# The first input of a two-network kernel made feature-major ahead of its scale and shift

## The chip, the core and the metric

One core of one Trainium2 chip runs the whole program. The metric is the device time of one execution in microseconds; the kernel before has a median of 1216.44 us over three runs (1214.46 to 1216.67). Everything is fp32; where the kernel multiplies at the faster rate it splits an operand into a high part (`hi`, type fp32r) and the rest (`lo`) and adds three products, `hi*hi + lo*hi + hi*lo`.

## The reference, cut to what matters

A token block of 256 rows and 1024 features goes through seven sublayers. Every sublayer has an input `h` that is a normalised `x`, scaled and shifted by vectors that come from a condition `c` through a 1024-row matrix:

```
shift, scale, gate = split(c @ mod_w[layer, 0] + mod_b[layer, 0], 3)
h = rms_norm(x, norm_w[layer, 0, 0]) * (1.0 + scale) + shift
y = mixer_ab(h, ...)      # first sublayer: h @ w_in, then two attentions
```

The change concerns only the first `h`: `x` is an input, and the scale and shift of this one sublayer (2 x 1024 columns of `mod_w`, 8 MB) have to be read and multiplied with `c` before any projection can start. The scales, shifts and gates of the later sublayers (a 1024 x 1024 matrix each) are made beside other work.

## The kernel before, in words

`start` makes the first `h`, feature-major: `hh` and `hl` (the high and low part) hold 8 blocks of 128 features by 256 tokens. It works in two halves q of 512 features (four blocks each), and in each half first on the scale (v = 0) and then on the shift (v = 1). Row kk of the matrix, as packed, is a 128 x 512 tile; eight rows make one vector half. `load(q, v, i)` brings four of them (i = 0 or 1) by two DMAs. Each row is either multiplied into `acc` by VectorE (`scalar_tensor_tensor`, line 1554) or multiplied on TensorE with `c` spread over 128 columns (`cb`, line 1551); `total` adds `acc` with a matrix of ones (line 1557). So scale and shift come as rows, spread over all partitions. `scaled` multiplies `x` with the scale (tokens on partitions); `shifted` adds the shift, turns the result by eight transposes per half (line 1579) and splits it into `hh` and `hl` (lines 187 and 188).

The first projection is the query of the second attention (`ab_qb`). It too works by halves: `prepare(i, t)` splits a quarter of the weights of half i into `whi` (ScalarE) and `wlo` (VectorE) through `split`; `run(i, t)` multiplies it, 12 products of 128x128 by 256 columns (lines 178 to 180). `run(0, t)` needs the first half of `h` alone, `run(1, t)` the second. The first is issued inside `start`, the second at the start of `mixer_ab`, followed by `ab_kb` and `ab_v` (`tok`), and then the softmax pipeline of the two attentions with further projections as filler. Beside it, in pieces, the gate of the first sublayer and the scale and shift of the second are summed: VectorE's `macc` (line 319), each piece with its own 1 MB DMA of `mod`.

What sets the order: TensorE's instructions run as the program writes them. All others are put in order when the program is built, by a scheduler that plays through estimated times; every engine then runs its list strictly in that order. `issue_after(a)` forbids the scheduler to place an instruction ahead of `a`. All DMAs go through SyncE's one list into one queue. Buffers `raw` (six, 1 MB each) and `whi`/`wlo` (four each) are used in turn.

Of the kernel before, what the change touches and what calls it, by code (L numbers as in the profile page):

```python
# [17 lines left out]
D = 1024  # L18
# [35 lines left out]
def packed(np, I):  # L54
# [75 lines left out]
    o["s5_b"], o["s5_cm"] = b.reshape(128, 1024), ct.reshape(128, 1024)  # L130
    o["mod_bias"] = np.concatenate([I["mod_b"].reshape(12, D), I["b_mod_2"].reshape(9, D)])
# [3 lines left out]
class Net:  # L135
    def __init__(self, ctx, tc, I, out, dbg=None):
        self.ctx, self.tc, self.nc, self.I, self.out, self.dbg = ctx, tc, tc.nc, I, out, dbg or {}
        self.bgq, self.late, self.wait = [], [], 0
        self.anchor = None
# [102 lines left out]
    def split(self, src, shape, pool=None):  # L242
# [13 lines left out]
        self.nc.scalar.activation(hv, src, AF.Copy)  # L256
        self.nc.vector.tensor_tensor(lv, src, hv.bitcast(F32), ALU.subtract)  # L257
# [592 lines left out]
    def mixer_ab(self, hh, hl):  # L850
        nc, I = self.nc, self.I
        with self.tc.tile_pool(name="ab", bufs=1) as ap:
            self.ap = ap
            Tb = [self.bias_load(h0, 3) for h0 in (8, 12)]
# [6 lines left out]
            nc.sync.dma_start(out=sink, in_=I["swa_sinks"][0].partition_broadcast(128))  # L861
# [17 lines left out]
            self.bgq = later  # L879
# [636 lines left out]
    def start(self):  # L1516
# [6 lines left out]
        with self.tc.tile_pool(name="start", bufs=1) as bp:  # L1523
            nw = bp.tile([1, D], F32, name="nw")
            ones = bp.tile([128, 128], F32, name="ones")
            nc.vector.memset(ones, 1.0)
            cb = bp.tile([128, 8, 128], F32, name="cb")
            nc.vector.tensor_copy(cb, self.c1.unsqueeze(2).to_broadcast([128, 8, 128]))
            hh, hl = self.h = self.h_tiles()
            rs = []  # L1530

            def load(q, v, i):

                if i == 0:
                    acc = bp.tile([128, 512], F32, name=f"acc{v}{q}")
                    mods[v] = self.bank([512]), acc, True
                    nc.gpsimd.memset(acc, 0.0)
                ps, acc = mods[v][:2]
                w = I["mod0"][q, v, i]
                r = self.raw() if i == 0 and not (q and v) else bp.tile([128, 2048], F32, name="sraw", bufs=5)  # L1540
                r = r.rearrange("p (k n) -> p k n", k=4)
                pairs = [r[:, 0:2], r[:, 2:4]]
                for k in range(4):
                    kk = 4 * i + k
                    r = pairs[k // 2][:, k % 2, :]
                    if k % 2 == 0:
                        nc.sync.dma_start(out=pairs[k // 2], in_=w[:, k:k + 2])
                        if kk == 0:
                            nc.sync.dma_start(out=acc[0:1, :], in_=I["mod_bias"][1 - v:2 - v, 512 * q:512 * q + 512])
                    if kk in (((1, 3, 5, 7), (1, 3, 5, 7)), ((3, 7), (3, 7)))[q][v]:  # L1550
                        nc.tensor.matmul(ps, cb[:, kk, :], r, start=mods[v][2], stop=False)
                        mods[v] = ps, acc, False
                    else:
                        nc.vector.scalar_tensor_tensor(acc, r, self.c1[:, kk:kk + 1], acc, ALU.mult, ALU.add)

            def total(v):
                nc.tensor.matmul(mods[v][0], ones, mods[v][1], start=False, stop=True)
                return mods[v][0]

            def scaled(q, ts):  # L1560

                sl = slice(512 * q, 512 * q + 512)
                ws = bp.tile([128, 512], F32, name="ws0", bufs=1)
                nb = self.bank([512])
                nc.tensor.matmul(nb, ones[0:1, :], nw[:, sl], start=True, stop=True)
                nc.scalar.activation(ws, nb, AF.Copy)
                nc.vector.scalar_tensor_tensor(ws, total(0), 1.0, ws, ALU.add, ALU.mult)
                for h in range(2):
# [157 lines left out]
```

## Time and profile before

| | |
|---|---|
| median of three runs | 1216.44 us |
| profiled execution | 1219.88 us, its span 1218.1 us |
| busy in the span | TensorE 95%, VectorE 76%, ScalarE 50%, GpSimd 11% |
| mean rate of the DMA queue | 248 GB/s over the span, 412 GB/s from 10 to 45 us |

The span is what the profiler sees between the first and the last instruction. Busy times of different engines overlap; an idle engine costs time only where the next engine waits for it. Matmuls are pipelined, so the length of one (0.28 us) is longer than the distance to the next (0.12 us).

### The profile page before, as it was taken

The page shows a single profiled execution, that of the slowest core. Times are in us where ns is not written, and L with a number is a line of the kernel's source. Part 1 is how long each engine was busy: PE and PEld are TensorE (multiplying, and loading weights), DVE is VectorE, ACT ScalarE, POOL GpSimd, SP SyncE. Part 2 cuts the span into 40 slices and gives each one's busy share as a digit, 9 for nine tenths or more (in the row PEclk, how much of TensorE's full clock was granted, in tenths as well). Part 3 has the DMA queues.
Part 4 walks back from the last instruction along what each step waited for, and adds up shares of the span by engine and source line. Part 5 has one row for each costly group of instructions (what it writes and reads, how often), then busy time and mean ns, then how long its engine had stood idle before and what let it go on. Part 6 is the DMA issues. An engine that isn't in the chain of part 4 may idle for free.

```text
span 1218.1 us, 19252 instructions
## 1 busy us (share of the span) xinstructions
PE 1158.5 (95%) x7460; PEld 1004.7 (82%) x7460; DVE 920.3 (76%) x1352; ACT 603.3 (50%) x1097; POOL 136.2 (11%) x181
## 2 busy tenths in 40 slices
PE   6997999999999999999999799999999889999997
PEld 2885469999878955999988699998888667999985
DVE  5897778877759796997796888777569958666545
ACT  2465545454445654554468764544343324445433
POOL 2000020000000012200000200000028850000000
PEclk9998999999999999999999899999999889999999
DMA  9975578867855768776987488688454534665530
GB/s 351 407 272 191 226 277 313 307 236 301 328 223 221 285 241 350 290 289 253 338 316 267 142 307 312 227 302 339 173 203 148 186 139 173 242 230 190 203 104 34
DMA packets 49537, 302.66 MB, mean 248 GB/s; under 512 B 6155, under 2 KB 6283, under 8 KB 16934
## 3 DMA queue, kind: packets, MB, share of 16 engines
q1 hardware_dynamic: 49446, 301.44, 66.3%
q8 instruction: 58, 0.95, 0.3%
q14 instruction: 33, 0.27, 0.1%
HBM read 295.64 MB, written 5.78 MB: 247 GB/s over the span
## 4 chain that ended last, share of the span: by engine, by line
PE 61%; issue 18%; DVE 10%; DMA 4%; ACT 3%; POOL 3%; POOLq 0%; SPq 0%; DVEq 0%; ACTq 0%
PE ps L180 11%; PE ps L178 11%; PE ps L179 11%; PE y L518 5%; PE y L516 5%; PE y L517 5%; PE y L514 4%; PE tok L546 2%; DMA sraw<-in_mod_dram 2%; DVE macc L319 2%; PE ps L1306 1%; DVE st L1358 1%; ACT p L676 1%; DVE wlo L257 1%; PE ps L432 1%
## 5 line engine op out<-in xcount | busy, mean ns | idle before, releaser
L256 ACT ACTIVATE whi<-raw 128x1024 fp32r<-128x1024 f32 (+2 forms) x307 | 318.1, 1045 | 375.4 <-PE ps L179 148.0
L257 DVE TENSOR_TENSOR wlo<-raw,whi 128x1024 fp32r<-128x1024 f32 (+2 forms) x307 | 370.1, 1211 | 162.8 <-ACT whi L256 161.3
L180 PE MATMUL ps<-hhi,wlo 128*128 128x256 f32 x1488 | 421.9, 284 | 3.4 <-DVE wlo L257 3.4
L178 PE MATMUL ps<-hhi,whi 128*128 128x256 f32 x1488 | 424.2, 285 | 0.0
L179 PE MATMUL ps<-hlo,whi 128*128 128x256 f32 x1488 | 421.5, 283 | 0.0
L180 PEld LDWEIGHTS ps<-hhi,wlo 128*128 128x128 f32 x1488 | 285.9, 192 | 4.4 <-DVE wlo L257 4.4
L178 PEld LDWEIGHTS ps<-hhi,whi 128*128 128x128 f32 x1488 | 285.9, 192 | 2.6 <-issue 1.4
L179 PEld LDWEIGHTS ps<-hlo,whi 128*128 128x128 f32 x1488 | 286.0, 192 | 1.4 <-DVE wlo L257 0.5
L319 DVE SCALAR_TENSOR_TENSOR macc<-raw,c,macc 128x1024 f32<-128x1024 f32 x152 | 194.6, 1280 | 2.4 <-issue 1.5
L516 PE MATMUL y<-whi,gh 128*128 128x512 f32 x352 | 139.6, 397 | 0.0
L518 PE MATMUL y<-whi,gl 128*128 128x512 f32 x352 | 139.1, 395 | 0.0
L517 PE MATMUL y<-wlo,gh 128*128 128x512 f32 x352 | 138.8, 394 | 0.0
L309 POOL MEMSET macc<- 128x1024 f32 x19 | 18.8, 989 | 589.5 <-DVE mlo L334 561.8
L518 PEld LDWEIGHTS y<-whi,gl 128*128 128x128 f32 x352 | 66.5, 189 | 15.4
L517 PEld LDWEIGHTS y<-wlo,gh 128*128 128x128 f32 x352 | 66.6, 189 | 15.2
L516 PEld LDWEIGHTS y<-whi,gh 128*128 128x128 f32 x352 | 66.6, 189 | 14.9
L514 PE MATMUL y<-raw,o 128*128 128x512 f32 x128 | 57.3, 595 | 0.2 <-ACT o L185 0.2
L617 DVE TENSOR_TENSOR g<-sg,ps 128x256 f32<-128x256 f32 x80 | 33.4, 418 | 29.1 <-PE ps L180 29.0
L399 POOL TENSOR_SCALAR ms<-ss 128x1 f32<-128x1 f32 x24 | 11.3, 472 | 372.3 <-ACT junk L409 368.4
L176 PE MATMUL ps<-h,raw 128*128 128x256 f32 x192 | 46.6, 400 | 5.0 <-DVE cvt L1436 5.0
L176 PEld LDWEIGHTS ps<-h,raw 128*128 128x128 f32 x192 | 38.1, 201 | 11.3 <-DVE cvt L1436 5.2
L514 PEld LDWEIGHTS y<-raw,o 128*128 128x128 f32 x128 | 23.4, 190 | 26.6 <-issue 25.6
(313 smaller groups left out, 1439.6 us busy)
## 6 DMA issues: line engine op xcount, KB each, us to landing
raw<-in_mod_dram SPq DMA_DIRECT2D x76, 1024.0 KB
raw<-in_ffn_g_dram SPq DMA_DIRECT2D x44, 1024.0 KB
raw<-in_ffn_u_dram SPq DMA_DIRECT2D x44, 1024.0 KB
raw<-in_ffn_d_dram SPq DMA_DIRECT2D x44, 1024.0 KB
raw<-in_ab_out_dram SPq DMA_DIRECT2D x8, 1024.0 KB
raw<-in_cd_out_dram SPq DMA_DIRECT2D x8, 1024.0 KB
raw<-in_s_c_dram SPq DMA_DIRECT2D x6, 1024.0 KB
raw<-in_s_out_dram SPq DMA_DIRECT2D x6, 1024.0 KB
```

The source lines that it names most:

```text
L176: mm(out, lh, rh, start=first, stop=last)
L178: mm(out, lh, rh, start=first, stop=False)
L179: mm(out, lh, rl, start=False, stop=False)
L180: mm(out, ll, rh, start=False, stop=last)
L256: self.nc.scalar.activation(hv, src, AF.Copy)
L257: self.nc.vector.tensor_tensor(lv, src, hv.bitcast(F32), ALU.subtract)
L319: nc.vector.scalar_tensor_tensor(acc, box["r"][:, kk % 2], c[:, kk:kk + 1], acc, ALU.mult, ALU.add)
L514: mm(ys[h][b], xh[:, k, c], wh[:, 0, sl], start=first, stop=last)
L516: mm(ys[h][b], xh[:, k, c], wh[:, 0, sl], start=first, stop=False)
L517: mm(ys[h][b], xh[:, k, c], wl[:, 0, sl], start=False, stop=False)
L518: mm(ys[h][b], xl[:, k, c], wh[:, 0, sl], start=False, stop=last)
L617: nc.vector.tensor_tensor(g, sg, pu, ALU.mult)
```

## The change

`x` is brought first. ScalarE scales it by its norm alone, TensorE turns it by 16 transposes into `xt` (feature-major) while the weights still arrive. The scale and shift are then wanted as columns: a row of weights is the stationary operand and `c` the moving one, so a product has one column, and four of them (128 features each) make one half. Three rows of eight go this way (`direct`), five are summed by VectorE (`rows`, the first a `tensor_scalar`), and `total` adds that sum with four more one-column products. The bias and the norm weight come as columns too (`cols0`). `modulated` applies scale and shift per partition: ScalarE writes `hh` (Identity with scale and bias), VectorE the same value into `t0` and the difference into `hl`. The splits of `ab_qb` are tied behind the last of these (`heads`). The bias tiles `Tb` and `sink` are loaded after item 4 of `mixer_ab`'s first chain, no longer at its head.

```
-        self.nc.scalar.activation(hv, src, AF.Copy)
-        self.nc.vector.tensor_tensor(lv, src, hv.bitcast(F32), ALU.subtract)
+        with ExitStack() as behind:
+            for a in self.heads:
+                behind.enter_context(self.tc.issue_after(a))
+            self.nc.scalar.activation(hv, src, AF.Copy)
+            self.nc.vector.tensor_tensor(lv, src, hv.bitcast(F32), ALU.subtract)
...
-            Tb = [self.bias_load(h0, 3) for h0 in (8, 12)]
...
                 if i == 4:
                     self.setup()
-            self.bgq = later
+                    nc.sync.dma_start(out=sink, in_=I["swa_sinks"][0].partition_broadcast(128))
+                    Tb = [self.bias_load(h0, 3) for h0 in (8, 12)]
+            self.bgq, self.heads = later, ()
...
+            def column(q, v, lhs, rhs, last=False):
+                for b in range(4):
+                    mm(sums[q][:, 4 * v + b:4 * v + b + 1], lhs[:, 128 * b:128 * b + 128], rhs, start=q not in first,
+                       stop=last and b == 3, skip_group_check=True)
...
+            def rows(q, v, ks):
+                for j, kk in enumerate(ks):
+                    r = parts[q, v, kk // 4][:, kk % 4]
+                    if j == 0:
+                        acc = parts[q, v] = bp.tile([128, 512], F32, name=f"acc{v}{q}")
+                        nc.vector.tensor_scalar(acc, r, self.c1[:, kk:kk + 1], None, ALU.mult)
+                    else:
+                        a = nc.vector.scalar_tensor_tensor(acc, r, self.c1[:, kk:kk + 1], acc, ALU.mult, ALU.add)
+                return a.ins
+            def direct(q, v, kk):
+                column(q, v, parts[q, v, kk // 4][:, kk % 4], self.c1[:, kk:kk + 1])
+            def total(q, v):
+                column(q, v, parts[q, v], one, v == 1)
+                m = bp.tile([128, 4], F32, name=f"m{v}{q}")
...
+            def modulated(q, ws, sh):
+                for b in range(4):
+                    k = 4 * q + b
+                    t = bp.tile([128, 256], F32, name="t0", bufs=3)
+                    nc.vector.tensor_scalar(t, xt[:, k], ws[:, b:b + 1], sh[:, b:b + 1], ALU.mult, ALU.add)
+                    a = nc.scalar.activation(hh[:, k], xt[:, k], AF.Identity, scale=ws[:, b:b + 1], bias=sh[:, b:b + 1]).ins
+                    self.anchor = nc.vector.tensor_tensor(hl[:, k], t, hh[:, k].bitcast(F32), ALU.subtract).ins
+                self.heads = a, self.anchor
...
+            for v in range(2):
+                rows(0, v, (0, 2, 4, 6, 7))
+                for kk in (1, 3, 5):
+                    direct(0, v, kk)
+                mods.append(total(0, v))
+            modulated(0, *mods)
...
-            with self.tc.issue_after(self.anchor):
-                early = {t: prepare(0, t) for t in range(4)}
-            load(1, 0, 0)
-            load(1, 0, 1)
+            early = {t: prepare(0, t) for t in range(4)}
+            fetch(1, 0)
+            fetch(1, 1)
             run(0, 0, early[0])
             run(0, 1, early[1])
-            scaled(1, tb)
-            load(1, 1, 0)
-            load(1, 1, 1)
+            sums[1] = self.bank([8])
+            a = self.anchor
+            for v in range(2):
+                with self.tc.issue_after(a):
+                    a = rows(1, v, (0, 2, 3, 5, 7))
+            direct(1, 0, 1)
             run(0, 2, early[2])
-            shifted(1, tb)
+            direct(1, 0, 4)
             run(0, 3, early[3])
+            direct(1, 0, 6)
+            mods = [total(1, 0)]
+            for kk in (1, 4, 6):
+                direct(1, 1, kk)
+            mods.append(total(1, 1))
+            modulated(1, *mods)
```

The order on VectorE around the moment when `h` is whole, before: `raw_337` is the second half of `ab_qb`, `raw_407` is `ab_kb`, `raw_439` and `raw_481` are `ab_v`, `raw_597` is the first piece of `mod`.

```order
L257 TENSOR_TENSOR wlo_340<-raw_337,whi_339 128x512
L257 TENSOR_TENSOR wlo_357<-raw_337,whi_356 128x512
L257 TENSOR_TENSOR wlo_374<-raw_337,whi_373 128x512
L1576 SCALAR_TENSOR_TENSOR t0_251<-t0_251,rstd_123,ps_256 128x512
L1576 SCALAR_TENSOR_TENSOR t0_253<-t0_253,rstd_132,ps_256 128x512
L188 TENSOR_TENSOR hlo_93<-ps_288,hhi_92 128x4x128
L1621 TENSOR_TENSOR iddup_447<-c32_155 128x128
L188 TENSOR_TENSOR hlo_93<-ps_296,hhi_92 128x4x128
L257 TENSOR_TENSOR wlo_391<-raw_337,whi_390 128x512
...
L257 TENSOR_TENSOR wlo_484<-raw_481,whi_483 128x816
L319 SCALAR_TENSOR_TENSOR macc_592<-raw_597,c1_80,macc_592 128x1024 x2
```

And of the change, where `raw_393` is the second half of `ab_qb` and `raw_658` the first piece of `mod`:

```order
L1588 TENSOR_SCALAR t0_373<-xt_98,m01_340,m11_359 128x256
L1590 TENSOR_TENSOR hlo_97<-t0_369,hhi_96 128x256
L1590 TENSOR_TENSOR hlo_97<-t0_373,hhi_96 128x256
L263 TENSOR_TENSOR wlo_396<-raw_393,whi_395 128x512
L1642 TENSOR_TENSOR iddup_503<-c32_88 128x128
L325 SCALAR_TENSOR_TENSOR macc_653<-raw_658,c1_80,macc_653 128x1024
L263 TENSOR_TENSOR wlo_413<-raw_393,whi_412 128x512
L263 TENSOR_TENSOR wlo_430<-raw_393,whi_429 128x512
```

All four splits of that weight half now stand behind the last `hlo`, and the first `macc` stands between the first and the second of them; before, it stood behind seven splits that follow `t0`.

TensorE's last steps ahead of the second half of `ab_qb`, of the change (`acc01` and `acc11` are VectorE's sums for scale and shift of q = 1, `ps_285` is where the columns add up):

```order
L1556 MATMUL ps_285<-c1_80,sraw_250 128x1 x4
L1556 MATMUL ps_285<-one_92,acc01_286 128x1 x4
L1556 MATMUL ps_285<-c1_80,sraw_253 128x1 x4
L1556 MATMUL ps_285<-c1_80,sraw_256 128x1 x8
L1556 MATMUL ps_285<-one_92,acc11_292 128x1 x4
L181 MATMUL ps_259<-hhi_96,whi_395 128x256
L182 MATMUL ps_259<-hlo_97,whi_395 128x256
L183 MATMUL ps_259<-hhi_96,wlo_396 128x256
```

Between the last `run(0, t)` and the first product of `run(1, t)` there are now 24 one-column products and no transposes.

## Rows read from the trace of the kernel before

**Rows 1.** The page, part 1: busy time, share of the span, instructions.

```profile
PE 1158.5 (95%) x7460; PEld 1004.7 (82%) x7460; DVE 920.3 (76%) x1352; ACT 603.3 (50%) x1097; POOL 136.2 (11%) x181
```

**Rows 2.** Busy time by stretch (us from the span's start).

```profile
core 0: us, PE busy (x) PEld busy (x) DVE busy (x) ACT busy (x) POOL busy (x), PEclk, DMA share, GB/s
0.00:10.00 10.00, 3.08 (x4) 1.00 (x4) 2.65 (x6) 1.28 (x1) 3.53 (x9) 1.00 0.71 228
10.00:45.00 35.00, 31.36 (x110) 16.70 (x109) 26.92 (x41) 11.89 (x24) 3.56 (x8) 0.90 1.02 412
24.90:31.70 6.80, 6.31 (x16) 3.70 (x17) 6.80 (x12) 0.60 (x2) 0.00 (x0) 0.50 1.04 418
41.85:74.60 32.75, 32.75 (x250) 32.12 (x249) 27.98 (x64) 21.06 (x47) 0.90 (x4) 1.00 0.95 378
76.50:100.10 23.60, 23.56 (x196) 21.56 (x196) 19.81 (x60) 9.35 (x30) 0.96 (x1) 1.00 0.59 213
103.40:113.60 10.20, 8.89 (x22) 4.31 (x22) 6.66 (x22) 6.02 (x22) 0.00 (x0) 0.50 0.67 257
```

**Rows 3.** TensorE in order of time: start, length, [idle before, releaser].

```profile
19.79 1.12 PE L1551 MATMUL ps<-sraw,cb 128*128 128x512 f32 x2 [0.16 <-DMA sraw<-in_mod_dram]
29.76 0.41 PE L180 MATMUL ps<-hhi,wlo 128*128 128x256 f32 x1
29.97 0.41 PE L178 MATMUL ps<-hhi,whi 128*128 128x256 f32 x1
40.72 1.38 PE L1579 MATMUL ps<-c,t 128*128 128x128 f32 x8 [1.18 <-DVE t L1576]
43.24 0.28 PE L180 MATMUL ps<-hhi,wlo 128*128 128x256 f32 x1
43.36 0.28 PE L178 MATMUL ps<-hhi,whi 128*128 128x256 f32 x1
45.01 0.28 PE L178 MATMUL ps<-hhi,whi 128*128 128x256 f32 x1
```

**Rows 4.** VectorE in order of time, around the moment when `h` is whole.

```profile
37.64 1.29 DVE L257 TENSOR_TENSOR wlo<-raw,whi 128x512 fp32r<-128x512 f32 x2
39.31 0.69 DVE L257 TENSOR_TENSOR wlo<-raw,whi 128x512 fp32r<-128x512 f32 x1 [0.38 <-ACT whi L256]
42.85 0.68 DVE L188 TENSOR_TENSOR hlo<-ps,hhi 128x512 fp32r<-128x512 f32 x1
44.15 0.69 DVE L257 TENSOR_TENSOR wlo<-raw,whi 128x512 fp32r<-128x512 f32 x1 [0.62 <-ACT whi L256]
51.25 1.28 DVE L319 SCALAR_TENSOR_TENSOR macc<-raw,c,macc 128x1024 f32<-128x1024 f32 x1
```

**Rows 5.** SyncE's queue: the first 1 MB piece of `mod` issued.

```profile
32.60 0.33 SPq L273 DMA_DIRECT2D raw<-in_mod_dram  x1
```

**Rows 6.** ScalarE in order of time: the first use of `x`.

```profile
14.07 0.63 ACT L409 ACTIVATE junk<-x 128x512 bf16<-128x512 f32 x1 [12.07 <-DMA x<-in_x_dram]
```

**Rows 7.** Line 974: ns min/median/max of one, first and last start.

```profile
L974 PE MATMUL ps<-ca,raw x32: 196/278/278, 88.7 to 92.1; 128*128 128x34 f32 x32
```

**Rows 8.** VectorE by line and shape (busy us, mean ns); and one timeline row.

```profile
L319 DVE SCALAR_TENSOR_TENSOR macc<-raw,c,macc 128x1024 f32<-128x1024 f32 x152 | 194.6, 1280 | 2.4 <-issue 1.5 <-DMA raw<-in_mod_dram 0.3
L643 DVE TENSOR_TENSOR gl<-g,gh 128x256 fp32r<-128x256 f32 x80 | 33.4, 418 | 0.0
L1554 DVE SCALAR_TENSOR_TENSOR acc<-sraw,c,acc 128x512 f32<-128x512 f32 x13 | 9.3, 747 | 1.2 <-DMA sraw<-in_mod_dram 1.1
L257 DVE TENSOR_TENSOR wlo<-raw,whi 128x512 fp32r<-128x512 f32 x8 | 5.2, 685 | 1.0 <-ACT whi L256 1.0
85.60 0.88 DVE L687 TENSOR_SCALAR p<-p,st 128x256 f32<-128x256 f32 x3
```

**Rows 9.** TensorE in order of time: its two longest waits from 41.85 to 110 us.

```profile
76.54 0.66 PE L694 MATMUL ps<-c,p 128*128 128x128 f32 x4 [1.56 <-ACT p L685]
104.23 1.19 PE L1023 MATMUL ps<-qa,kc 128*128 128x256 f32 x2 [3.89 <-ACT kc L999]
```

More of the change, by code (lines that the diff above doesn't have):

```diff
@@ L130, in packed @@
     o["s5_b"], o["s5_cm"] = b.reshape(128, 1024), ct.reshape(128, 1024)
+    feat = lambda v: v.reshape(8, 128).T
+    o["cols0"] = np.concatenate([feat(I["norm_w"][0, 0, 0]), *(feat(I["mod_b"].reshape(12, D)[1 - v]) for v in range(2))], 1)
     o["mod_bias"] = np.concatenate([I["mod_b"].reshape(12, D), I["b_mod_2"].reshape(9, D)])
@@ L1523, in start @@
         with self.tc.tile_pool(name="start", bufs=1) as bp:
[L1524 to L1568, printed above, removed]
-                    t = bp.tile([128, 512], F32, name="t0", bufs=4)
-                    nc.vector.tensor_tensor(t, self.x[:, h, sl], ws, ALU.mult)
-                    ts.append(t)
@@ L1582, in start @@
-            mods, ta, tb = {}, [], []
-            load(0, 0, 0)
-            load(0, 0, 1)
-            nc.sync.dma_start(out=self.x, in_=I["x"][0].rearrange("(h p) d -> p h d", p=128))
-            nc.sync.dma_start(out=nw, in_=I["norm_w"][0, 0, 0:1])
-            self.neghalf = cp.tile([128, 4], F32, name="neghalf")
-            nc.vector.memset(self.neghalf, -0.5)
-            for h in range(2):
-                rs.append(self.rstd(*self.mean_sq([self.x[:, h, 512 * q:512 * q + 512] for q in range(2)], D)))
@@ L1595, in start @@
             self.ident = self.c32[:, C_ID:C_ID + 128]
-            load(0, 1, 1)
+            cols = bp.tile([128, 24], F32, name="cols")
+            nc.sync.dma_start(out=cols, in_=I["cols0"])
+            one = bp.tile([128, 1], F32, name="one")
+            nc.vector.memset(one, 1.0)
+            self.neghalf = cp.tile([128, 4], F32, name="neghalf")
+            nc.vector.memset(self.neghalf, -0.5)
+            hh, hl = self.h = self.h_tiles()
+            mm = nc.tensor.matmul
+            xt = bp.tile([128, 8, 256], F32, name="xt")
@@ new lines, in start, with fetch @@
+            sums, parts, first = {}, {}, set()
+            def fetch(q, v):
+                for i in range(2):
+                    r = self.raw() if i == 0 and not (q and v) else bp.tile([128, 2048], F32, name="sraw", bufs=5)
+                    parts[q, v, i] = r = r.rearrange("p (k n) -> p k n", k=4)
+                    for k in (0, 2):
+                        nc.sync.dma_start(out=r[:, k:k + 2], in_=I["mod0"][q, v, i][:, k:k + 2])
+            def column(q, v, lhs, rhs, last=False):
+                for b in range(4):
+                    mm(sums[q][:, 4 * v + b:4 * v + b + 1], lhs[:, 128 * b:128 * b + 128], rhs, start=q not in first,
+                       stop=last and b == 3, skip_group_check=True)
+                    first.add(q)
```

34 lines of the change are left out of this document (19 added, 15 removed).

## The prediction, made before the changed kernel ran

> **What bounds the kernel now.** The page comes first: TensorE is busy for 95% of the span, so what keeps TensorE waiting costs time one for one [rows 1]. The view of stretches then shows where that holds: from 41.85 to 74.60 us TensorE is busy all the time, and from 76.50 to 100.10 for 23.56 of 23.60 us [rows 2]. Ahead of 41.85 us it is another kernel: the DMA engines are full (share 1.02 from 10 to 45 us, 412 GB/s) and TensorE waits, for data or for VectorE [rows 2, 3]. So only two moments of the start count: when the first input `h` is whole, which lets the second half of the first projection (four groups `run(1, t)` of 12 products) begin, and whether TensorE is fed from then on. Before, the last matmul ahead of that ends at 43.24, `run(1, 0)` begins at 43.36 and `run(1, 1)` at 45.01 us [rows 3]. A microsecond that TensorE loses after that shifts the end, except where it waits anyway: 1.56 us at 76.54 and 3.89 us at 104.23 [rows 9].
>
> VectorE's timeline says why it was fed: three of the four weight halves that `run(1, t)` needs (`wlo`, 128x512) were split at 37.64 to 39.31, while the shift was still being summed; only the fourth came after the last `hlo` at 42.85. The first piece of the next modulation vector (`macc`) ran at 51.25, behind them all [rows 4].
>
> **First half of `h` (q = 0).** The last weights of (0,1) are there at 19.79 us as before [rows 3]: the bytes queued ahead of them are the same, `x` only went to the front. VectorE now takes both last rows itself, 2 x 0.75 us from the row of L1554 [rows 8], to 21.3 us. Then come four products of one column, two passes each. Nothing in the trace has one column; the nearest row is the 34-column product: 32 passes from 88.7 to 92.1 us, 0.11 us each, 0.22 a product, at the full clock [rows 7]. At the half clock I take double, 0.44; a floor is zero, as the passes could hide beside waiting. That is 0.9 to 1.8 us, to 22.2 to 23.1. The new scaling and splitting is four TENSOR_SCALAR at 0.88/3 = 0.29 us and four TENSOR_TENSOR at 0.42 on 128x256 [rows 8], 2.8 us at most, against two transposed blocks before; ScalarE works beside it. One short row and a 0.69 us split later the first full triple of products runs, at about 26.3 us, where before it was at 29.76 [rows 3]. The head start is 3.4 us.
>
> **Second half (q = 1).** The weights are issued in the same order, and VectorE has ten rows and four splits from 25.5 us on, 10 x 0.75 + 4 x 0.69: it is through by 35.8 us. TensorE is later. It has 48 products of `run(0, t)` and 32 column products (three rows and a total for each of two vectors, four columns each) to do in order before the shift is summed; before, `run(0, 3)` stood behind the transposes. From 26.3 us: half the products at the low rate, 24 x 0.21 (29.76 to 29.97), half at the high one, 24 x 0.12 (43.24 to 43.36) [rows 3], and 32 x 0.22: 5.1 + 2.9 + 7.0 = 15.0, to 41.3 us. Add 0.3 for the small rows and 2.8 for scaling and splitting: `h` is whole at 44.4, against 43.5 before (42.85 + 0.68 [rows 4]). The head start of 3.4 us is used up by columns and by `run(0, 3)`. Bounds: with columns that cost nothing `h` comes 7 us sooner, at half clock throughout 9 us later (C below). The 0.9 us itself does not show in the sum, because of what comes next.
>
> **What is queued behind it.** Since `heads` orders the splits of `ab_qb`'s second half behind `h`, all four now follow it. The order on VectorE is first split, `iddup`, `macc`, second split: the first multiply-accumulate of the next modulation vector stands ahead of the weights of `run(1, 1)`, and it needs its 1 MB piece of `mod`. That piece is the first after `cmp` in the queue in both kernels. The sizes up to its end, by the shapes in SP's order and in MiB: `x` 1, `consts` 0.2, `mod0` 8, `ab_qb` 2, `ab_kb` 0.5, `wbc` 0.5, `ab_v` 1.6, `ab_cmp` 1 and the piece 1, in all 16.59 MB. The queue moved 2.28 MB by 10 us (228 GB/s), and does 412 GB/s after [rows 2]: 10 + 14.31/0.412 = 44.7 us. To this comes the lag to the last engine's share: before, `x` ended at 3.15 MB, so 12.1 us by this sum, and ScalarE was released by it at 14.07 [rows 6]. So the piece is there at 46.7 us, though it was issued at 32.60 [rows 5]. Before, nobody asked until 51.25. Now VectorE stands on it from about 45.4 (44.4 + 0.69 + 0.28): 46.7 + 1.28 + 0.69 [rows 8] = 48.7 for the second `wlo`. `run(1, 1)`, whose third product needs it, is in effect at 48.4 instead of 45.01: **+3.4 us** for TensorE, and the scores, softmax and everything else wait behind. Bounds: were the start of the queue at 412 GB/s too (from 2 us), the piece would come 2.5 us sooner and this term is +0.9; the other end is +4. I take the row's rate, since the first transfers are as long as before.
>
> **The clock.** TensorE idles about 3.4 us there, after a stretch of one-column products. The granted clock was 0.50 from 24.9 to 31.7 us, after a stretch with waits, and from 103.4 to 113.6 us, after the 3.89 us wait [rows 2, 9]; at 0.50, 1.2 GHz, a product takes 0.21 instead of 0.12. Of the first stretch about 3.2 us were dense work (28.5 to 31.7), of the second about 5; half of that is lost, 1.6 to 2.5 us. I take **+2.1**, bounds 0 and +4.
>
> **What comes back.** VectorE does three more `macc` (3 x 1.28) ahead of the first softmax than before, so the 1.56 us for which TensorE waited on the softmax at 76.54 should go: **-1.6**, bounds 0 and -1.6 (the wait is no longer) [rows 9]. The bias tiles still follow the `mod` piece in SP's queue, and are wanted more than 5 us after they land: nothing. `wbc` now lands ahead of `v`, 1.3 us of transfer; `v` is wanted 9 us later: nothing. POOL's four memsets of 128x512 fall away beside idle time: nothing.
>
> Sum: 3.4 + 2.1 - 1.6 = **+3.9 us**, 1219.9 to 1223.8 us for an execution under the profiler, with 1.8 us around its span of 1218.1. The median of the unprofiled runs, 1216.44, lies 3.4 below that; the same step gives **1220.3 us**.
>
> **Rivals.** A, *faster: VectorE's relief is worth more than its stall.* The queue fills at once, so the piece is there at 44.2 us and `h` before it; `run(1, 1)` then starts at 44.2 + 1.28 + 0.69 - 0.24 = 45.9, 0.9 us late, too little to drop the clock. From there VectorE is 3 x 1.28 = 3.8 us ahead, and both waits of TensorE behind the softmax, 1.56 and 3.89 us [rows 9], shrink by as much in all: 0.9 - 3.8 = -2.9, 1213.5. It decides once the piece lands before 44.7 us. For it: VectorE is busy for 27.98 of the 32.75 us in question [rows 2]. Against it: nothing in the change makes the first transfers faster, and the wait at 104.23 is put down to ScalarE. The Trainium skill (VectorE: DVE Perf Modes, Mode 2x_2P) has fp32 TENSOR_SCALAR out of SBUF at two results a cycle; the four in front of `h` would then take 0.15 and not 0.29 us each and `h` would come 0.6 us sooner, which helps A alone. The row of L687 does not show it: 0.88 us for three of 256 columns.
>
> B, *absorbed.* VectorE blocks, but the clock stays high and TensorE's later waits (1.56 and part of 3.89) take up most: 3.4 - 1.6 - 1 = +0.8, 1217.2. Against it: TensorE has no other gap between 41.85 and 100 us.
>
> C, *slower by far: columns at half clock.* If one-column work does not raise the clock, `run(0, t)` and the columns all go at 1.2 GHz: 48 x 0.21 + 32 x 0.44 = 24.2, the shift at 50.5 and `h` at 53.6 us. `macc` then waits for nothing, and it is 53.6 - 43.5 = +10.1, +2.1, -1.6: +10.6, 1227.0. It decides once `h` comes after 47 us. For it: before, the clock was at 0.50 to 31.7 us although 512-column products ran. Against it: between 26.3 and 31 us the 256-column products are dense, as they were when the clock rose, and the 34-column products from 88.7 us on ran at 1.00 throughout [rows 2, 7]. The Trainium skill (TensorE: Matmul & The Clock Gate, A second HAM failure mode: psum-queue depth-cycling) says that short idle moments between groups of matmuls are enough to make the clock swing; by it C would be likelier than I make it, by the 34-column row less likely.
>
> **Chances.** Forecast 0.48, A 0.20, B 0.18, C 0.14. About 0.2%, 2.4 us, is what this measurement can tell from no change. A is faster; B is the same, and so is a twentieth of the forecast: faster 0.20, same 0.20, slower 0.60. The forecast alone gives 1217.5 to 1223 (wait 2.6 to 4, clock 0 to 4). The range for 8 in 10 reaches to A and to C: 1213.5 to 1227.
>
> **What would show it.** Right: VectorE idle ahead of the first `macc`, released by a DMA, near 46.7 us; `run(1, 1)` near 48.4; a granted clock of 0.50 around 50 us; TensorE's wait at the first transposes of softmax gone. Wrong: `macc` without idle time ahead of it, or `run(1, 1)` before 46 us (A); `h` after 47 us (C); or the attention ending at the same time as before although `run(1, 1)` is late (B). The forecast fails altogether if the mean of one column product is far from 0.22 us at the full clock.

## The result

The changed kernel has a median of 1224.12 us (1221.98 to 1225.93), the kernel before, run beside it, of 1216.44 us: ratio 1.0069, 95% interval 1.0057 to 1.0082. It is 7.7 us slower. The profiled execution took 1223.75 us with a span of 1222.0.

TensorE in order of time, where before it ran [rows 3] (start, length, [idle before, releaser]):

```profile
13.91 3.41 PE L1556 MATMUL ps<-c,raw 128*128 128x1 f32 x16
18.89 1.85 PE L1556 MATMUL ps<-one,acc 128*128 128x1 f32 x8
20.99 3.57 PE L1556 MATMUL ps<-c,raw 128*128 128x1 f32 x16 [0.25 <-DVE m L1579]
26.13 1.85 PE L1556 MATMUL ps<-one,acc 128*128 128x1 f32 x8
30.91 0.58 PE L181 MATMUL ps<-hhi,whi 128*128 128x256 f32 x1 [2.94 <-ACT whi L262]
35.94 0.95 PE L1556 MATMUL ps<-c,raw 128*128 128x1 f32 x8
36.75 0.36 PE L181 MATMUL ps<-hhi,whi 128*128 128x256 f32 x1
42.69 3.31 PE L1556 MATMUL ps<-c,sraw 128*128 128x1 f32 x24 [0.26 <-DVE m L1579]
45.86 1.84 PE L1556 MATMUL ps<-one,acc 128*128 128x1 f32 x8
50.65 0.58 PE L181 MATMUL ps<-hhi,whi 128*128 128x256 f32 x1 [2.94 <-ACT whi L262]
54.96 0.36 PE L181 MATMUL ps<-hhi,whi 128*128 128x256 f32 x1
55.16 0.28 PE L182 MATMUL ps<-hlo,whi 128*128 128x256 f32 x1
```

The 128x1 rows are the one-column products; "x8" is four products in two passes each. Between 13.91 and 27.97 us TensorE does nothing else: 64 passes, one after the other, 0.21 to 0.22 us a pass. At 35.94 us, in between dense products, eight passes take 0.81 us, 0.10 each. So the first stretch goes at the half rate, and that is read from the pitch (the distance from one start to the next): the column of the granted clock, PEclk, has 1.00 from 10 to 28 us, but this trace has no record of the clock ahead of its rise at 34.6 us, and the column counts what has no record as full. The first half of `h` therefore lets `run(0, 0)` begin at 30.91 us (before: 28.55), and the second lets `run(1, 0)` begin at 50.65 instead of 43.36. The slow pitch lasts to 55 us.

VectorE, where before it ran [rows 4], and SyncE's queue at the same time:

```profile
28.01 0.16 DVE L1579 SCALAR_TENSOR_TENSOR m<-ps,cols 128x4 f32<-128x4 f32 x1 [6.88 <-PE ps L1556]
47.74 0.16 DVE L1579 SCALAR_TENSOR_TENSOR m<-ps,cols 128x4 f32<-128x4 f32 x1 [4.91 <-PE ps L1556]
50.63 0.69 DVE L263 TENSOR_TENSOR wlo<-raw,whi 128x512 fp32r<-128x512 f32 x1
51.44 1.28 DVE L325 SCALAR_TENSOR_TENSOR macc<-raw,c,macc 128x1024 f32<-128x1024 f32 x1
52.63 1.29 DVE L263 TENSOR_TENSOR wlo<-raw,whi 128x512 fp32r<-128x512 f32 x2
```
```profile
36.92 0.33 SPq L279 DMA_DIRECT2D raw<-in_mod_dram  x1
50.72 0.33 SPq L1645 DMA_DIRECT2D pf<-in_cmp_pe_dram  x1
```

VectorE, the engine that was relieved of work, stands idle for 6.88 and 4.91 us and is released by the one-column products each time. `macc` at 51.44 has no idle time ahead of it, and TensorE does not wait behind it: from 50.65 to 55 us it is busy without a break. SyncE issues nothing from 37 to 50.7 us: it waits 13.4 us for the last `hlo`, as its next tile takes memory that the start gives back then. The view of stretches shows that as an empty queue, and the low clock beside it (columns as in [rows 2]):

```profile
10.00:28.00 18.00, 17.28 (x79) 16.32 (x77) 6.85 (x12) 5.04 (x9) 0.15 (x1) 1.00 1.03 413
45.00:50.00 5.00, 2.70 (x13) 2.62 (x13) 2.22 (x8) 2.00 (x5) 0.00 (x0) 0.50 0.01 5
50.00:55.00 5.00, 4.35 (x19) 4.13 (x20) 5.00 (x11) 3.45 (x7) 0.90 (x4) 0.50 0.44 116
55.00:60.00 5.00, 5.00 (x43) 5.00 (x43) 4.52 (x7) 3.50 (x7) 0.00 (x0) 0.99 1.03 423
```

TensorE's two waits of before [rows 9] have become these:

```profile
84.32 0.66 PE L700 MATMUL ps<-c,p 128*128 128x128 f32 x4
111.46 1.97 PE L1029 MATMUL ps<-qa,kc 128*128 128x256 f32 x8 [0.26 <-issue]
```

Setting the start of each product against that of the same product before gives the lag along the program. It is +7.3 us at `run(1, 0)` (50.65 - 43.36), +9.3 at 46 us (the low clock: 2.0 more), +7.8 behind 76.54 us (the wait of 1.56 us is gone), up to +10.9 near 99 us, +3.9 at 125 us, and +6.4 from 134 to 450 us. In the profiled executions 2.5 us of this, net, go again at 690 to 706 and 960 to 1003 us, where the products of before ran longer at the half rate (granted clock from 680 to 700 us: 0.76 before, 0.84 after). The profiled execution of before, 1219.88 us, is 3.4 above its median, that of the change is at its median: +3.9 there, +7.7 between the medians.

### The profile page after: what moved, and what is told of

Read it like the earlier page. It is cut to its first block, busy times and chain, and to the rows that moved or that the text cites. A ratio compares the mean times of both kernels' runs of the same rounds, so it can differ in the third digit from the quotient of the medians.

```text
span 1222.0 us, 19436 instructions
## 1 busy us (share of the span) xinstructions
PE 1158.6 (95%) x7552; PEld 1021.9 (84%) x7552; DVE 914.4 (75%) x1359; ACT 609.3 (50%) x1107; POOL 133.1 (11%) x177
## 4 chain that ended last, share of the span: by engine, by line
PE 60%; issue 18%; DVE 11%; POOL 4%; ACT 4%; DMA 3%; SPq 0%; POOLq 0%; DVEq 0%; ACTq 0%
PE ps L183 11%; PE ps L181 11%; PE ps L182 11%; PE y L524 5%; PE y L522 5%; PE y L523 5%; PE y L520 4%; DVE macc L325 2%; PE tok L552 2%; DVE wlo L263 1%; PE ps L1312 1%; DVE st L1364 1%; ACT p L682 1%; POOL xt L1356 1%; DMA raw<-in_ab_qb_dram 1%
## 5 line engine op out<-in xcount | busy, mean ns | idle before, releaser
L179 PE MATMUL ps<-h,raw 128*128 128x256 f32 x192 | 45.6, 394 | 5.0 <-DVE cvt L1442 5.0
```

Source lines behind the costliest of these rows:

```text
L179: mm(out, lh, rh, start=first, stop=last)
```

## The experiments

Two theories. **L**: `h` is late because TensorE does the one-column products in its fixed order, at the half rate, and the clock does not rise under them. **S**: it is late, or `run(1, t)` is, because the splits are tied behind `h` and stand around `macc` on VectorE (the forecast's term among them). In the table, "lag" is measured as above, in us; the medians stand beside runs of the kernel before on the same chip, 1216.08 to 1217.56 us.

| kernel | run(0,0) | run(1,0) | lag at 74.6 | lag at 134 | median, us | ratio to before |
|---|---|---|---|---|---|---|
| the change | 30.9 | 50.7 | +9.3 | +6.4 | 1224.12 | 1.0057 to 1.0082 |
| e1 rows on VectorE | 26.5 | 45.4 | +4.0 | +4.3 | 1220.89 | 1.0024 to 1.0049 |
| e2 filler last | 30.9 | 52.9 | +12.5 | +9.4 | 1226.58 | 1.0062 to 1.0092 |
| e3 splits not tied | 29.0 | 49.3 | +9.1 | +4.5 | 1219.65 | 1.0015 to 1.0040 |
| e4 32 columns | 31.2 | 50.9 | +9.8 | +7.5 | 1228.31 | 1.0087 to 1.0120 |
| e5 macc later | 30.9 | 53.5 | +12.2 | +9.3 | 1226.48 | 1.0064 to 1.0093 |
| e6 bias first | 30.8 | 50.5 | +9.7 | +7.9 | 1232.94 | 1.0097 to 1.0138 |
| e7 columns ahead, tied | 26.5 | 48.1 | +8.4 | +10.5 | 1228.42 | 1.0082 to 1.0111 |
| e8 columns ahead, free | 24.1 | 47.6 | +6.2 | -0.8 | 1217.77 | 0.9995 to 1.0017 |
| e9 row form | 28.5 | 52.7 | +10.9 | +8.0 | 1227.81 | 1.0081 to 1.0115 |
| e10 VectorE, free | 23.9 | 44.0 | +2.9 | +0.6 | 1221.32 | 1.0030 to 1.0056 |
| e11 row form, free | 26.3 | 45.6 | +5.4 | -0.2 | 1214.83 | 0.9981 to 0.9999 |
| e12 row form, filler last | 26.5 | 46.9 | +4.1 | +0.9 | 1217.89 | 1.0000 to 1.0022 |

Starts and lags come from one profiled execution of each kernel, and the moment at which the clock rises in it moves `run(1, 0)` by up to 3 us (e5 below), so a difference of 1 or 2 us between two of them decides little. For nine of the thirteen kernels the lag at 134 us is the difference of the medians to within 1.8 us. The medians of e4, e6, e9 and e10 lie 3.7 to 8.2 us further from that of before than this lag: in the profiles of e6, e9 and e10 1.7 to 1.9 us of that come between 460 and 490 us, where the granted clock falls to 0.50 and that of before and of the change does not; the rest is open.

**e1, all rows on VectorE.**

```
-                rows(0, v, (0, 2, 4, 6, 7))
-                for kk in (1, 3, 5):
-                    direct(0, v, kk)
+                rows(0, v, range(8))
...
-                    a = rows(1, v, (0, 2, 3, 5, 7))
+                    a = rows(1, v, range(8))
...
-            direct(1, 0, 1)      # and the five others of q = 1
```

> All eight rows of every vector are summed by VectorE; TensorE keeps only the totals (32 of the 128 one-column steps of 16 products... 4 products for each vector). Theory L (the second half of h is late because one-column products stand in TensorE's order at the low rate): VectorE needs 16 rows from 9.7 us, at 0.75 each, to about 21.5; the total 1.9 more, the first half of h at 26 and run(0,0) near 26.5 instead of 30.9; VectorE then has 16 rows and four splits, 14.5 us, to about 40.5, total 1.9, scaling and splitting 2.9: run(1,0) near 45.5 instead of 50.65, a gain of 5 us, 1219 us, or 1217 if the low clock behind it goes too. Theory S (it is late because the weight splits are tied behind h): run(0,0) and run(1,0) move by under 1.5 us, 1223 us. The recorded forecast's own step: with h whole at 45 the first macc now does wait, until the 1 MB piece is there at 46.6, and run(1,1) starts near 48.3; that eats about 2 us of the gain: 1221.

TensorE in order of time:

```profile
26.45 0.58 PE L181 MATMUL ps<-hhi,whi 128*128 128x256 f32 x1 [2.94 <-ACT whi L262]
40.57 1.87 PE L1556 MATMUL ps<-one,acc 128*128 128x1 f32 x8 [4.19 <-DVE acc L1568]
45.37 0.58 PE L181 MATMUL ps<-hhi,whi 128*128 128x256 f32 x1 [2.94 <-ACT whi L262]
82.82 0.66 PE L700 MATMUL ps<-c,p 128*128 128x128 f32 x4 [3.85 <-ACT p L691]
```

Both starts are where theory L puts them (26.5 and 45.5 expected), to 0.2 us, and the two waits of 2.94 us for the splits, S's evidence, are as long as ever. Of the 5.3 us won at the lag of 74.6, 3.8 are lost again at 82.82: the first softmax is not ready, and TensorE waits 3.85 us where it waited 1.56 in [rows 9] and not at all in the change. The median gains 3.2 us. `macc` did not block here: the scheduler put the splits of `ab_qb` and `ab_kb` ahead of it, and it ran at 50.66.

**e2, e7 and e8: the columns put together, dense products kept as filler.** e2 only moves the columns of (1,0) ahead of `run(0, 2)` and those of (1,1) ahead of `run(0, 3)`:

```
-            direct(1, 0, 1)
-            run(0, 2, early[2])
...
+            for kk in (1, 4, 6):
+                direct(1, 0, kk)
+            mods = [total(1, 0)]
+            run(0, 2, early[2])
+            for kk in (1, 4, 6):
+                direct(1, 1, kk)
+            mods.append(total(1, 1))
+            run(0, 3, early[3])
```

> Only TensorE's order is changed: the columns and the total of (1,0) stand ahead of run(0,2), those of (1,1) ahead of run(0,3). Nothing is removed. Theory L: the totals are ready as soon as VectorE's rows are (37.1 and 40.4 us); total (1,0) ends near 38.5, run(0,2) to 40, columns and total of (1,1) at the full rate to 43.2, and run(0,3) runs beside scaling and splitting: run(1,0) near 46.3 instead of 50.65, and the wait of 2.94 us shrinks to about 1.5, so that the clock stays high: 4.4 + up to 2 gained, 1218 to 1220 us. Theory S: the 2.94 us of splits behind h stay whatever the order, run(1,0) no earlier than 49 and the clock low after it: 1222 to 1224 us.

It came out slower than both theories had it, and no faster than the change (1.0077 of the time before, the change 1.0069). The columns of (1,1) went at 0.21 us a pass throughout, 5.11 us for 24 where the change took 3.31, and `run(0, 3)` behind them was slow too:

```profile
37.96 1.93 PE L1556 MATMUL ps<-c,sraw 128*128 128x1 f32 x16
43.15 5.11 PE L1556 MATMUL ps<-c,sraw 128*128 128x1 f32 x24
52.91 0.58 PE L181 MATMUL ps<-hhi,whi 128*128 128x256 f32 x1 [0.18 <-ACT whi L262]
```

e8 does without columns in the first half, stands the second half's beside `run(0, 2)`, unties the splits (`self.heads = a, self.anchor` left out) and ties the first `macc` behind the first split of `ab_v`. e7 is the same with the splits tied and `macc` as in the change.

```
+            direct(1, 0, 1)
+            direct(1, 0, 4)
+            direct(1, 0, 6)
             run(0, 2, early[2])
+            for kk in (1, 4, 6):
+                direct(1, 1, kk)
+            mods = [total(1, 0)]
             run(0, 3, early[3])
+            mods.append(total(1, 1))
```

> As e7_early_h_tied, but the splits are not tied behind h and the first macc is tied behind the first split of ab_v. Theory L: run(0,0) near 25, h whole near 41.5, and run(1,0) begins with its first chunk near 40.5 instead of 50.65 (before: 43.36); VectorE has nothing in front of ab_kb's split. From there 2 to 3 us ahead of the kernel before, less what the low clock takes: 1213 to 1216 us. If the start of h is not what sets the end: 1219 us or more, with run(1,0) at 41 all the same.

> VectorE takes all eight rows of the first half; in the second half the six columns stand ahead of the totals, beside run(0,0) to run(0,2), and run(0,3) behind the total of the scale. The splits stay tied behind h, and the first macc stands ahead of all four of them. Theory L: run(0,0) at 26.5; VectorE's ten rows and four splits to 36.5, the totals at 39, h whole near 42, 8.5 us sooner than in the change. The recorded forecast's mechanism, here where h comes before the piece: VectorE stands on macc until 46.6, then 1.28 and the split 0.69: run(1,0)'s third product at 48.6 and the clock low behind it: 1221 to 1223 us though h is whole 8 us sooner. Rival (the piece is there in time or macc does not block): run(1,0) at 42.5, 1216 us.

The first half came as expected (24.1 and 26.5), the second did not: 47.6 and 48.1 instead of 40.5 and 42.5. e8's TensorE shows why:

```profile
31.81 1.93 PE L1557 MATMUL ps<-c,sraw 128*128 128x1 f32 x16
34.27 0.29 PE L183 MATMUL ps<-hhi,wlo 128*128 128x256 f32 x1
34.39 0.38 PE L181 MATMUL ps<-hhi,whi 128*128 128x256 f32 x1
34.57 0.41 PE L182 MATMUL ps<-hlo,whi 128*128 128x256 f32 x1
35.64 5.11 PE L1557 MATMUL ps<-c,sraw 128*128 128x1 f32 x24
45.02 1.70 PE L1557 MATMUL ps<-one,acc 128*128 128x1 f32 x8
```

24 one-column passes run at 0.10 us from 31.0 us, TensorE is never idle, and at 34.4, within dense products, the pitch goes from 0.12 to 0.21 (granted clock 1.00 from 31.0 to 34.4 us, 0.50 from there to 51.5). All columns behind cost double. In e7 `macc` ran at 48.05, when `h` was whole and the piece had landed; its own 1.28 us put the first split back and TensorE waited 1.07 us for it. A `macc` that waits for its piece in front of the splits, as the forecast described it, was seen in no run.

**e4, 32 columns instead of one.**

```
-                mm(sums[q][:, 4 * v + b:4 * v + b + 1], lhs[:, 128 * b:128 * b + 128], rhs, start=...
+                mm(sums[q][:, 4 * v + b, :], lhs[:, 128 * b:128 * b + 128], rhs.to_broadcast([128, 32]), start=...
```

> Each one-column product gets 32 equal columns as its moving operand (c's column repeated), and the first of the 32 results is used. Theory L with activity as the cause of the low clock: with 32 columns TensorE is granted 2.4 GHz as it was for the 34-column products at 88.7 us, a product falls from 0.44 to 0.22 us, total (0,1) is summed near 23 instead of 28 us and that of (1,1) near 41 instead of 47.7: run(1,0) 4 to 6 us sooner, 1218 to 1220 us. Rival (a 32-column product does no more for the clock than a one-column product): the same low rate, 0.43 to 0.5 us a product, run(1,0) at 50 to 52 us, 1223 to 1226 us.

The rival's case: 32 columns cost what one costs and leave the clock as low (the median is 2 us above its range, with the start where the change has it: 1.7 us are lost at the first softmax, where the lag grows from 9.8 to 11.5).

```profile
14.04 3.46 PE L1556 MATMUL ps<-c,raw 128*128 128x32 f32 x16
38.74 0.98 PE L1556 MATMUL ps<-c,sraw 128*128 128x32 f32 x8
```

0.21 us a pass at the low clock, 0.10 to 0.12 at the high one, as with one column. So up to 32 moving columns cost nothing of their own; what every pass has is the load of its 128x128 weights, and these loads stand one behind the other (PEld 16.32 of the 18 us from 10 to 28 us in the change). The Trainium skill (TensorE: Matmul & The Clock Gate, LDWEIGHTS) gives a weight load as the number of its columns over 1.2, in ns: 107 ns for 128. The trace bears that out at 2.4 GHz (0.10 us a pass from 35.94 us); at the granted 1.2 GHz it has twice that (0.21 from 45.86 us).

**e3, splits not tied; e5, macc later.** e3 leaves out `self.heads = a, self.anchor`; e5 adds a tie:

```
                 if i == 4:
+                    self.anchor = self.low      # wlo of the first split of ab_v
                     self.setup()
```

> The weight splits are no longer tied behind h, neither in the first half nor in the second; VectorE and ScalarE may do them in the 6.9 and 4.9 us in which VectorE idles. Theory S: both waits of 2.94 us of TensorE shrink by about 2 us each, and since the second adds to the first run(1,0) comes about 4 us sooner, near 46.6, 1219 to 1220 us. Theory L: the first half gains 2 us, but the end of the columns of (1,1) is set by TensorE's order and its low rate, so that about 1.5 to 2 us come in the first half, 2 in the second at the most: run(1,0) near 48, 1221 us. The recorded forecast (3.4 us for macc between the splits): 1220.7 us with macc waiting for its piece, but no one behind it.

> The change as it is, but the first macc is tied behind the first split of ab_v instead of the last hlo; the four splits of ab_qb's second half, those of ab_kb and the first of ab_v come ahead of it. Recorded forecast: its term of 3.4 us and the clock's 2.1 go, 1218 to 1219 us. Theory L: the piece has landed at 46.6, four us before h is whole, so macc delays the second split only by its own 1.28 us, which is ahead of its use; run(1,0) and run(1,1) stay at 50.65 and near 53.2, and the time stays at 1223 to 1225 us but for the order on VectorE behind it.

e3 took the waits of 2.94 us down to 0.95 and 0.89, yet `run(1, 0)` moved by 1.3 us alone. That looks like L, but it does not decide: in this execution the granted clock falls at 42.4 us, in the change at 44.9, so that the 24 passes for (1,1) take 4.86 us instead of 3.31 and `h` is whole at 51.4, later than in the change. With the change's 5.0 us from the first of these passes to the end of the total, `run(1, 0)` would be at 47.8 (an estimate), between S (46.6) and L (48). The median, 1219.65, is what S had (1219 to 1220). The lag of 9.1 at 74.6 is nearly that of the change; between 75 and 134 us it falls by 1.7 us more than there. The rest of the 4.5 us between the medians is not in this profile: its execution, 1224.9 us, is the longest of ten. In e5 the four splits of `run(1, t)` no longer have `macc` among them:

```profile
53.50 0.58 PE L181 MATMUL ps<-hhi,whi 128*128 128x256 f32 x1 [2.94 <-ACT whi L262]
```
```profile
53.48 0.69 DVE L263 TENSOR_TENSOR wlo<-raw,whi 128x512 fp32r<-128x512 f32 x1
54.29 1.29 DVE L263 TENSOR_TENSOR wlo<-raw,whi 128x512 fp32r<-128x512 f32 x2
```

Nothing was won; the forecast's term is not what the change costs. That `run(1, 0)` is at 53.5 and not at 50.65 has another reason: the instructions up to there are those of the change in the same order, but the clock rises at 37.7 instead of 34.6 us (`run(0, t)` is at the pitch of 0.12 us from 38.3 on), and the columns of (1,1) are slow from 44.5 on.

**e6, bias tiles first.** The bias tiles and sinks at the head of `mixer_ab`, as before:

```
+            Tb = [self.bias_load(h0, 3) for h0 in (8, 12)]
             o8 = ap.tile([128, 8, 256], F32, name="o8")
...
-                    Tb = [self.bias_load(h0, 3) for h0 in (8, 12)]
```

> One part undone: the two bias tiles and the sinks are loaded at the head of mixer_ab again. Recorded forecast: the place of the bias tiles is worth nothing, 1224 us, the same start of run(1,0) at 50.65. Rival: they stand ahead of ab_qb's successors and the mod pieces in SP's queue, and wait for the memory that the start gives back, so that the pieces behind them come later: 1225 to 1228 us. A gain below 1222 us speaks against both.

The start is the same (50.45) and the time 1232.94: slower even than the rival had it. TensorE waits at places where the change does not:

```profile
86.09 0.33 PE L700 MATMUL ps<-c,p 128*128 128x128 f32 x1 [1.46 <-ACT p L691]
166.02 10.57 PE L520 MATMUL y<-raw,o 128*128 128x512 f32 x24 [2.23 <-ACT o L188]
```

By 160 us the lag is 3.6 us above that of the change. The profiled execution, 1228.38 us, is 4.6 below the median of its runs; where the rest goes is open. By this run the later bias tiles are a gain within the change, which the forecast put at nothing.

**e9 to e12: the row form.** TensorE's three rows as one product each of 512 columns, with `c`'s column stationary; ScalarE copies the summed row out of PSUM, and four products of one partition turn it into columns:

```
-                column(q, v, parts[q, v, kk // 4][:, kk % 4], self.c1[:, kk:kk + 1])
+                mm(lines[q, v][0:1, :], self.c1[:, kk:kk + 1], parts[q, v, kk // 4][:, kk % 4], ...)
...
+                nc.scalar.activation(row, lines[q, v][0:1, :], AF.Copy)
+                column(q, v, row, one[0:1, :])
```

> Only the form of TensorE's share is changed: each of its three rows of a vector is one product of 512 columns with c's column stationary, summed as one row in PSUM (ScalarE copies it out, four one-column products of one partition turn it). One-column products fall from 128 to 64 in all. Theory L (narrow products are dear and let the clock fall): a row costs 0.43 to 0.85 us instead of 0.8 to 1.76; the shift of the first half is there near 22.5 instead of 28.0, run(0,0) near 25.5 instead of 30.9, run(1,0) near 43 to 45 instead of 50.65; 1217 to 1219 us. If the form does not matter (what counts is that TensorE does these rows at all in its order): run(0,0) no earlier than 28, run(1,0) no earlier than 48, 1221 to 1224 us.

> As e9_row_form, with the rows of (1,1) ahead of the totals, the splits not tied behind h and the first macc behind the first split of ab_v: the version that the runs so far point to. Theory L: run(0,0) near 24, VectorE through with ten rows and eight splits at about 37, h whole near 41, run(1,0) near 40 to 41 instead of 43.36 in the kernel before; 1212 to 1215 us. If the start of h does not set the end, or the low clock takes it all: 1217 us or more with run(1,0) at 41.

e9 gained 2.5 us in the first half and lost 4.5 in the second: before each total TensorE waits for ScalarE's copy, and four of the six passes for the rows of (1,1) go at half the rate (4.43 us for six). e11 has all products of rows ahead of both totals, the splits free and `macc` later:

```profile
40.52 1.05 PE L1557 MATMUL ps<-one,row 1*128 1x1 f32 x8 [0.74 <-ACT row L1581]
42.48 4.43 PE L1575 MATMUL ps<-sraw,c 128*1 128x512 f32 x6
```
```profile
35.17 1.88 PE L1576 MATMUL ps<-sraw,c 128*1 128x512 f32 x4
38.60 1.88 PE L1576 MATMUL ps<-sraw,c 128*1 128x512 f32 x4
40.41 1.05 PE L1558 MATMUL ps<-one,acc 128*128 128x1 f32 x8
45.61 0.58 PE L181 MATMUL ps<-hhi,whi 128*128 128x256 f32 x1 [0.89 <-ACT hhi L1597]
```

(The first fence is e9, the second e11.) In e11 the granted clock is full from 31.8 to 45.5 us; a row costs 0.9 us, not the 0.43 expected at best, hardly different from four one-column products (0.8), and so `run(1, 0)` came at 45.6 and not at 40 to 41. It is the fastest kernel of all, 0.999 (0.9981 to 0.9999) of the time before, which is hardly a gain, though its second half of `h` is later than there: from 74.6 to 134 us its lag falls from +5.4 to -0.2.

e10 has no columns but the totals, with e8's two ties; e12 is e11 with `run(0, 3)` moved behind both totals.

> As e1_rows_on_vector (no columns but the totals), with the splits not tied behind h and the first macc behind the first split of ab_v. Against e8_early_h_free it tells whether the 24 columns of the second half, bunched behind run(0,2), are what kept h at 49 there. Theory L: run(0,0) at 24, VectorE is through with rows and splits at about 42, total 1.9, run(1,0) with its first chunk near 44, with e1's at 45.4: 1216 to 1219 us. If the order on VectorE is what counts and not the columns: run(1,0) at 47 as in e8, 1218 us or more.

> As e11_row_form_free, in another order on TensorE: three rows of (1,0) and one of (1,1) ahead of run(0,2), the other two behind it, then both totals, and run(0,3) behind these as work for the time in which the second half of h is scaled and split. Theory L: the totals end near 41 instead of 44.7 and run(0,3) covers 1.5 of the 2 us behind them; run(1,0) near 43 instead of 45.6, and the clock may stay at 2.4 GHz (2 us more): 1211 to 1214 us. Rival, from e2_filler_last and e8_early_h_free (the totals bunched without dense work between them let the clock fall before run(0,3)): run(0,3) at 0.21 us a product, run(1,0) near 46 and slow, no gain on e11: 1215 to 1218 us.

e10 bears out L for the start (44.0; e8, with the columns, 47.6), but its median, 1221.32, is above L's range. It meets the first softmax with 3.85 us of waiting, as e1, yet by 134 us its lag is only +0.6: its time is lost later, and but for 1.7 us at 460 to 490 us it is open where. So the start of `h` does not set the time alone: e10 has the earliest, e11 starts 1.6 us later and is 6.5 us faster. e12 went as its rival said: the clock fell during the totals (at 41.9 us), and the filler ran at half rate.

```profile
41.16 1.25 PE L1558 MATMUL ps<-one,acc 128*128 128x1 f32 x8 [0.26 <-DVE m L1587]
42.34 1.86 PE L1558 MATMUL ps<-one,row 1*128 1x1 f32 x8
44.73 0.41 PE L183 MATMUL ps<-hhi,wlo 128*128 128x256 f32 x1
```

## Why the prediction was right, and where its steps were not

The direction and the range held (forecast 1220.3, slower, 1213.5 to 1227; measured 1224.12), but not for the reason given: by its own signs (`h` after 47 us, `macc` without idle time ahead of it) the forecast's mechanism was wrong. The time lies in the range because the range was drawn as far as C; C's 1227.0 is 2.9 us away, the forecast's own figure 3.8. That the two profiled executions differ by 3.9 us, just the sum, is chance: the lag was 6.4 us at 134 us, and 2.5 of it went where the profiled execution of before was itself slow.

- **First half of `h`, first full triple at 26.3: failed.** `run(0, 0)` began at 30.91, the triple at 32.06. VectorE had its last sum at 20.1 us, sooner than the 21.3 counted. The step counted only the four products behind the last row. It left out that the 28 other products of the half stand ahead of them in TensorE's order, at the rate that it had itself put at 0.44 us: 64 passes from 13.91 to 27.97. At 0.10 us a pass, as at 35.94 us, they would have taken 6.4 us and been through with VectorE at about 21 (an estimate). e1, without 24 of the 32 products, has `run(0, 0)` at 26.45, with the same wait of 2.94 us for the splits. From the end of the total to the triple it took 4.1 us, 3.65 were counted.
- **Second half, 15.0 us of TensorE's work: mis-sized.** From 30.91 to 47.70 it took 16.8 us, as the clock fell again among the columns at 44.9. With the late first half (4.6 us) that makes `h` whole at 50.7 instead of 44.4.
- **The price of a column: right.** 0.43 to 0.44 us at 1.2 GHz, 0.20 at 2.4 GHz (0.44 and 0.22 estimated). The trace of before had a nearer row than the 34 columns: four passes of two columns (L1405) from 979.84 to 980.20 us, 0.09 us each.
- **VectorE blocked at `macc`, +3.4: failed.** The 1 MB piece had landed by 46.4 us (46.7 forecast; the queue moves nothing from 46.0 on), but `h` came later still, so nothing waited for it. In its place stands the late `h` itself, +7.3 us at `run(1, 0)`. That is rival C's sign (`h` after 47 us, `macc` without idle time ahead) and its cause, columns at half rate, but not its working: C had `run(0, t)` and the columns behind it at half rate throughout, 24.2 us, and they took 16.8, as the clock rose at 34.6. Of the 6.3 us by which `h` is later than forecast 4.6 come from the first half, which C took over from the forecast as it stood. C was given 0.14, and one reason against it was wrong. That the 34-column products from 88.7 us ran at the full clock [rows 7] says little: in the change the same products run from 96.5 us, TensorE is not idle, and the granted clock falls at 99.5 and stays at 0.50 to 106.3. The Trainium skill (TensorE: Matmul & The Clock Gate, A second HAM failure mode: psum-queue depth-cycling), by which C was likelier, speaks of short idle moments. The clock did fall, but not in that way: TensorE is not idle when it falls in e8.
- **The clock, +2.1: right in size, not in cause.** The lag grows from 7.3 to 9.3 us while the pitch is 0.21 (50.65 to 55 us). But the clock had not fallen behind a wait, as the step had it: it fell at 44.9 us among the columns, with TensorE busy.
- **The wait at 76.54, -1.6: right in size.** It is gone (84.32); lag 9.3 to 7.8. That VectorE's three more `macc` are the reason is not shown: with two more than before, e1 and e10 wait 3.85 us there.
- **What was priced at nothing.** Between 85 and 134 us the lag changes by another -1.4 us net, the sum of four larger pieces that the traces show. It rises by 3.1 to 99 us, where the change has its half clock from 99.5 to 106.3 us. It falls by 3.6 at 104.23, where the wait of 3.89 us is gone but for 0.26 (A and B counted on that, the sum did not), and by 3.3 to 125 us, most of it where before had its half clock, 103.4 to 113.6 us [rows 2]. It rises by 2.5 to 134 us, where the change has its half clock again (133.6 to 137.0 us). By e6 the place of the bias tiles matters; the first was wanted as it landed (VectorE waited 0.29 us for it at 58.2 us), not 5 us later. The queue that runs empty from 46.0 to 51.7 us was not foreseen; what it costs was not isolated.

The change's half clock behind 99.5 us, in the view of stretches (columns as in [rows 2]):

```profile
90.00:100.00 10.00, 10.00 (x85) 9.86 (x84) 5.90 (x28) 6.84 (x25) 0.95 (x1) 0.97 0.31 122
100.00:110.00 10.00, 10.00 (x60) 7.69 (x61) 9.68 (x28) 4.23 (x16) 0.00 (x0) 0.68 0.82 312
```

So 7.3 + 2.0 - 1.5 - 1.4 = +6.4 us at 134 us, against a sum of +3.9.

Shown: that the columns in TensorE's order make `h` late (VectorE's waits of 6.88 and 4.91 us end with them; e1, and e10 against e8), and that `macc` among the splits does not (TensorE has no wait behind it in the change; e5). Shown only in part is what each costs in time. By the lag at 134 us the change has +6.4, without columns (e1) +4.3, without the tie of the splits (e3) +4.5, without both and with `macc` later (e10) +0.6: the tie, S's part, costs there about as much as the columns. The medians, 7.7, 4.8, 3.5 and 5.2 us above before, say the same of e1 and e3, but not of e10.

Not explained is what the attention between 74.6 and 134 us does with a late start. The change, e2, e3, e5, e8, e9, e11 and e12 gain 3 to 7 us there; for the change the pieces are given above, for the others they were not followed. The number of `macc` that VectorE has behind it at the first softmax does not decide it: it is four before, five in e12 (gains 3.2), six in e1 (loses 0.3), e2 (gains 3.1), e4 and e10, and seven in the others, of which e8 gains 7.0 and e7 loses 2.1.

## What to carry to other kernels

A product with few columns costs its weight load, here 0.20 or 0.44 us: count it in TensorE's order from the first to the last, at the rate of that stretch, before VectorE's relief is counted. Small groups of such products between dense ones (four products in the change, 35.9 to 41.2 us) ran at the high rate; put together (e2, e7, e8), they were followed by the low clock, which the dense work behind them then paid. And read what the next phase does with a head start or a delay before it is priced: here 2 to 7 us of it went again in the attention's waits and its stretches of low clock.

## What the runs showed of the chip

- In these runs narrow products did not keep the clock up, though TensorE had no idle time: in e8 the pitch of the 256-column products fell from 0.12 to 0.21 us at 34.4 us, after 24 one-column passes and six dense products; in e2, e7 and e12 it fell likewise (in e12 behind a wait of 0.26 us). Widening them to 32 columns changed nothing (e4). After 32 passes of 34 columns the clock fell in the change (at 99.5 us), but not in the kernel before (1.00 from 76.5 to 100.1 us [rows 2]).
- The change, e5 and e6 have the same instructions on TensorE, VectorE and ScalarE up to `h`, and saw the clock rise at 34.6, 37.7 and 35.7 us. `run(1, 0)` came at 50.7, 53.5 and 50.5 us: up to 3 us without any edit to this part.
- Products of 512 columns with one stationary column take 0.45 to 0.47 us a pass at the high rate (e11, from 35 to 40 us) and about twice that at the low one (e9, from 42.6 to 46.0 us). Between dense products they went with the full granted clock from 31.8 us on in e11; it fell at 45.5, behind the 32 one-column passes at the end.
